# Split operands for the state's product in the chunk scan of a pooling and Mamba-2 step

## The chip, the cores and the metric

The kernel runs on one core of one Trainium2 chip, as one launch. The metric is the device time of that launch in microseconds (us). The core has a matrix engine (TensorE, PE in the profile), a vector engine (VectorE, DVE), an activation engine (ScalarE, ACT), a general engine (GpSimd, POOL) and an engine that here only issues DMAs (SyncE, SP). Each works through its own queue in order, and they meet at semaphores. Tiles lie in SBUF on 128 partitions; PE writes its products to PSUM banks of 128 x 512 float32 numbers.

## The reference

One layer of a hybrid decoder, for a prompt of 1024 rows and for 8 samples of 8 rows, 1024 wide. A normalised and modulated input goes through one projection; its parts feed a pooling branch and a state-space (SSD) branch, whose outputs are gated, summed and projected. The change lies in the SSD branch of the prompt. It has 32 heads of 64 channels in 4 groups of 8 heads; each group shares B and C (128 states). The 1024 rows are scanned in 8 chunks of 128:

```python
def step(h, inp):
    xq, dq, Bq, Cq = inp
    acs = jnp.cumsum(dq * Ag, axis=1)
    seg = acs[:, :, None] - acs[:, None, :]
    decay = jnp.exp(jnp.where(mask, seg, -jnp.inf))
    cb = jnp.einsum('bign,bjgn->bijg', Cq, Bq)
    att = cb[..., None] * decay * dq[:, None]
    y = jnp.einsum('bijge,bjgep->bigep', att, xq)
    y = y + jnp.einsum('bign,bige,bgepn->bigep', Cq, jnp.exp(acs), h)
    last = acs[:, -1]
    w_in = jnp.exp(last[:, None] - acs) * dq
    h = h * jnp.exp(last)[..., None, None] + jnp.einsum('bjgn,bjge,bjgep->bgepn', Bq, w_in, xq)
    return h, y
...
y = (y + d_skip.astype(jnp.float32)[:, None] * xs).reshape(b, L, D_INNER)
y = rmsnorm(y * jax.nn.silu(z_ssm.astype(jnp.float32)), ssm_norm_g)
s = y.astype(x.dtype) @ w_ssm_out
```

The state after the last chunk is an output too.

## The kernel before

All large products are made in split form: a float32 operand becomes a high part in the type fp32r and a low part, the rest, and the product is the sum of high x high, low x high and high x low. ACT makes the high part by a copy, DVE or GpSimd the low part by a subtraction.

**Stages.** The input is normalised, transposed and modulated (to about 90 us). Then the input projection runs in pairs of column tiles by a Strassen scheme (products on line 411, to about 758 us); beside it GpSimd and ACT split later weights, the convolution runs on DVE (line 1089), dt and its cumulative sums are made in `dt_end` (lines 1104 to 1205), and the 8 samples are scanned. The chunk stage follows (about 758 to 1045 us), then the last group's output products and the last projection with the final norm.

**The chunk stage.** 32 generators `chunk(g, c)` (line 1492), 4 groups by 8 chunks, one after the other. Each goes through five steps:

1. It issues its loads: `dec`, the cumulative sums of the group's 8 heads spread over all partitions; `bc` (B and C); `xb` (x, 4 tiles of 128 channels by 128 rows).
2. ACT makes `cE` (exponentials of the sums, line 1504), GpSimd masks `dec` (`far`, line 1229), and ACT turns it into decays, one instruction a head with the row's own sum as bias (`exps`, line 1233).
3. PE transposes x into the bank `px` (line 1511) and B into `pbc`, and makes the product of B and C there (lines 1513, 1514). ACT copies B's transpose to `bt` and, after the first chunk, C into PSUM (line 1518). DVE makes `xd` = x dt (line 1522) and `xw` = x weighted for the state (line 1524), and multiplies `dec` and `cE` by PSUM (lines 1529, 1531).
4. PE makes the state's increment `pu` = bt x xw (line 1536), a plain float32 product of 128 x 128 by 128 x 512, then `inner` (lines 1245, 1248): 8 heads of decays against `xd` and, after the first chunk, of `cE` against the state before. GpSimd decays the state (line 1542) and DVE adds `pu` (line 1544). DVE adds D x to the result in PSUM, four instructions with a scale for each channel (line 1548).
5. `finish` (line 1462): DVE multiplies by the gate `sz` (line 1464), ACT makes the high part and the squares, GpSimd the low part (line 1468) and sums of squares.

**Order.** The loop on line 1844 hands out the steps: in iteration i step 3 of chunk i + 1, some products, step 4 of chunk i, the loads of chunk i + 3 and of the gate, step 2 of chunk i + 2, step 5 of chunk i, one step of `wo_splits` (which splits the last projection's weights, lines 1766 to 1819), and more products. The products are 2.56 pieces an iteration of other branches' output projections (`gemm_`, line 221, 12 matmuls of 352 or 384 columns a piece, added up on DVE in line 1740 after the first group). From line 1834 on `in_line` fixes the program's order on PE and SP (at the start of the stage on ACT and DVE too); a scheduler with a timeline of its own orders ACT, DVE and GpSimd. `xw` has one buffer, `xd` and `bt` two, `xb` five, `sz` three; four PSUM banks (`PB`) go round for `px`, `pbc` and `inner`, and `pu` has one of its own (`PC`).

The functions that the change touches, and what calls them:

Of the kernel before, what the change touches and what calls it, by code (L numbers as in the profile page):

```python
# [8 lines left out]
F32 = mybir.dt.float32  # L9
F32R = mybir.dt.float32r  # L10
AF = mybir.ActivationFunctionType
# [9 lines left out]
P = 128  # L21
# [25 lines left out]
def tile_pool_ssd_step(  # L47
# [8 lines left out]
    def nm(s):  # L56
        uid[0] += 1
        return f"{s}_{uid[0]}"
# [1045 lines left out]
    def dt_end():  # L1104
# [86 lines left out]
        for c0 in (8, 0, 4):  # L1191
            cs = range(c0, min(c0 + 4, 9))
            n = sum(P if c < 8 else NS for c in cs)
            ps = PB()
            for c in cs:
                m = P if c < 8 else NS
                nc.tensor.transpose(ps[:NH, (c - c0) * P:(c - c0) * P + m], acT[:m, c, :], ident[:m, :m])
            if c0 == NC:
                Es[0] = sp.tile([P, 2, 512], F32, tag="h0", name="E", bufs=H0B)[:NH, 0, :NS]
                V.tensor_copy(Es[0], ps[:NH, :n])  # L1200
                store_(acS_d.rearrange("b h t -> h b t"), Es[0].rearrange("h (b t) -> h b t", t=8))
            else:
                at = sp.tile([P, 512], F32, tag="xd", name=nm("at"), bufs=2)[:NH]
                V.tensor_copy(at[:, :n], ps[:NH, :n])
                store_(acs_d[c0:c0 + 4].rearrange("c h t -> h c t"), at.rearrange("h (c t) -> h c t", t=P))

# [24 lines left out]
    def exps(dec, g, c):  # L1231
        for h in range(8):
            act(dec[:, h], dec[:, h], AF.Exp, bias=acT[:, c, 8 * g + h:8 * g + h + 1], scale=-1.0)  # L1233
# [225 lines left out]
    def ckt(shape, tag, bufs=2):  # L1459
        return (cl if tag in CKL else ca if tag in ("dec", "xb", "cE", "bc") else ck).tile(list(shape), F32, tag=tag, name=nm(tag), bufs=bufs)  # L1460
# [26 lines left out]
    def load_sz(j):  # L1487
        g, c = divmod(j, NC)
        szs.append(ckt([P, 4, P], "sz", 3))
        load(szs[-1], z_d[g][:, :, c * P:c * P + P])  # L1490

    def chunk(g, c):
# [6 lines left out]
        xb = ckt([P, 4, P], "xb", 5)  # L1499
# [15 lines left out]
        bt = ckt([P, P], "bt", 2)  # L1515
        act(bt, pbc[:, :P], AF.Copy)
        if c > 0:
            act(pbc[:, 2 * P:3 * P], Cf, AF.Copy)
# [3 lines left out]
        V.tensor_tensor(xd, pxv, dtT[:, c, heads].unsqueeze(2).to_broadcast([P, 8, 64]), ALU.mult)  # L1522
        xw = ckt([P, 8, 64], "xw", 1)
        V.tensor_tensor(xw, pxv, wdT[:, c, heads].unsqueeze(2).to_broadcast([P, 8, 64]), ALU.mult)
        if g == c == 0:
            yield
            far(dec, c)
            exps(dec, g, c)
        V.tensor_tensor(dec, dec, pbc[:, P:2 * P].unsqueeze(1).to_broadcast([P, 8, P]), ALU.mult)
# [6 lines left out]
        mm(pu, bt, xw.rearrange("p h d -> p (h d)"), start=True, stop=True)  # L1536
# [10 lines left out]
        for q in range(4):  # L1547
            V.scalar_tensor_tensor(pi[:, q], xb[:, q], Dv[:, 4 * g + q:4 * g + q + 1], pi[:, q], ALU.mult, ALU.add)
        yield
        finish(g, o, P, xb, szs.pop(0), pi)  # L1550
# [59 lines left out]
    def to_ssd():  # L1610
        nonlocal right, sd, sp, mask, maskS, blkS, dtT, acT, wdT, Elb, ElS
# [9 lines left out]
        Elb, ElS = one([P, NC, NH], "Elb"), one([P, NB, NH], "ElS")  # L1621
# [6 lines left out]
    sd = sp = mask = maskS = blkS = dtT = acT = wdT = Elb = ElS = None  # L1628
# [75 lines left out]
    for shape, tag, bufs in (((P, 512), "ph", 3), ((P, P), "bt", 2), ((P, 8, 64), "xd", 2), ((P, 8, 64), "xw", 1),  # L1704
                             ((P, 4, NS), "szs", 1), ((P, 512), "t2", 1), ((P, 512), "hst", 2)):
        ckt(shape, tag, bufs)
# [576 lines left out]
```

## Time and profile before

| what | us |
|---|---|
| median of 3 runs | 1211.38 |
| lowest and highest run | 1211.2, 1212.2 |
| the profiled execution | 1210.91 |
| its span, first to last instruction | 1209.2 |

The profile is of one execution. A page of it has the busy time of each engine, the chain of waits followed back from the last instruction, and groups of instructions. A group's row reads: line, engine, operation, output<-inputs, shapes, count | busy us, mean ns of one | idle time of the engine before them and what ended it. A row of the timeline reads: start us, duration us, engine, line, operation, tiles, shapes, count. The rows of one line give the least, median and largest duration in ns, and first and last start. Matmuls are pipelined and their ends are modelled: what one costs is the distance to the next start. PEld is the weight load beside PE.

### The profile page before, as it was taken

The numbers are of one execution on the slowest core, as the hardware profiler recorded it, in microseconds if no ns is written. First come the engines' busy times: TensorE is split into PE (matmuls) and PEld (weight loads), VectorE is DVE, ScalarE is ACT, GpSimd is POOL, SyncE is SP. The second block draws the span as 40 slices with busy tenths as digits, with TensorE's granted clock in tenths as the row PEclk, the third lists the DMA queues.
The fourth block names the chain that finished last, engine by engine and source line by source line (L and its number), as shares of the span: only waits on it lengthen the run. The fifth ranks groups of instructions, "written<-read, shape, count | busy, mean of one in ns | idle before, by whom it ended". The sixth has DMA issues, their size and how long they took to land.

```text
span 1209.2 us, 25239 instructions
## 1 busy us (share of the span) xinstructions
PE 1194.4 (99%) x9242; PEld 1118.5 (93%) x9242; DVE 924.8 (76%) x1535; ACT 649.1 (54%) x1479; POOL 763.4 (63%) x655
## 2 busy tenths in 40 slices
PE   9999999999999999999999999999999999999997
PEld 8879999999999999999989999988888888999885
DVE  6993788877989578877576555687878889679976
ACT  6864356565666557454434334566676657312435
POOL 1137878875988787764777776255767758423653
PEclk9999999999999999999999999999999999999999
DMA  9836445574556455454667767988879888585794
GB/s 352 306 132 219 136 144 184 164 228 146 171 174 198 160 164 172 135 169 131 208 227 238 245 223 247 320 309 262 270 250 294 277 284 285 173 326 166 235 212 154
DMA packets 167924, 262.72 MB, mean 217 GB/s; under 512 B 32880, under 2 KB 80760, under 8 KB 167800
## 3 DMA queue, kind: packets, MB, share of 16 engines
q1 hardware_dynamic: 90408, 166.01, 41.9%
q10 hardware_dynamic: 73232, 87.16, 21.2%
q0 software_dynamic: 4160, 7.94, 3.2%
q8 instruction: 73, 1.20, 0.4%
q14 instruction: 51, 0.42, 0.1%
HBM read 173.31 MB, written 87.73 MB: 216 GB/s over the span
## 4 chain that ended last, share of the span: by engine, by line
PE 87%; DVE 5%; DMA 3%; ACT 2%; issue 1%; POOL 0%; ACTq 0%; DVEq 0%; SPq 0%; POOLq 0%
PE mm L411 24%; PE ps L411 23%; PE mm L221 17%; PE pc L411 5%; PE ps L1245 3%; PE pc L1536 2%; PE ps L1248 2%; PE ps L2036 2%; PE ps L2034 2%; PE ps L2035 2%; PE ps L1511 1%; DMA dec<-acs_d 1%; DMA Y<-in_x_prompt 1%; PE ps L957 1%; DVE tf L643 1%
## 5 line engine op out<-in xcount | busy, mean ns | idle before, releaser
L148 POOL TENSOR_TENSOR wlo<-rawA,whi 128x512 fp32r<-128x512 f32 x120 | 174.7, 1461 | 80.7 <-ACT whi L145 79.4
L221 PE MATMUL mm<-Y,whi 128*128 128x352 f32 (+1 forms) x960 | 195.9, 334 | 0.8 <-DVE G L1969 0.6
L148 POOL TENSOR_TENSOR wlo<-raw,whi 128x512 fp32r<-128x512 f32 x90 | 149.8, 1673 | 64.6 <-ACT whi L145 62.2
L221 PEld LDWEIGHTS mm<-Y,whi 128*128 128x128 f32 x960 | 159.2, 188 | 7.6 <-issue 4.1
L1089 DVE SCALAR_TENSOR_TENSOR GA<-GA,cvT,GA 128x1112 f32<-128x1112 f32 x72 | 134.0, 1866 | 0.1
L411 PE MATMUL mm<-Y,whi 128*128 128x272 f32 x800 | 118.4, 290 | 0.0
L145 ACT ACTIVATE whi<-rawA 128x512 fp32r<-128x512 f32 x120 | 75.1, 627 | 79.6 <-PE ps L411 34.7
L411 PE MATMUL ps<-Y,whi 128*128 128x272 f32 x800 | 117.4, 289 | 0.0
L145 ACT ACTIVATE whi<-raw 128x512 fp32r<-128x512 f32 x90 | 56.0, 629 | 103.9 <-DVE raw L348 34.0
L411 PEld LDWEIGHTS mm<-Y,whi 128*128 128x128 f32 x800 | 106.9, 188 | 2.5 <-issue 1.0
L411 PEld LDWEIGHTS ps<-Y,whi 128*128 128x128 f32 x800 | 107.0, 188 | 0.8 <-issue 0.7
L221 PE MATMUL mm<-Y,wlo 128*128 128x352 f32 (+1 forms) x480 | 98.5, 327 | 0.0
L1233 ACT ACTIVATE dec<-dec,acT 128x128 f32<-128x128 f32 x256 | 78.8, 389 | 25.8 <-POOL dec L1229 25.8
L221 PEld LDWEIGHTS mm<-Y,wlo 128*128 128x128 f32 x480 | 81.7, 188 | 0.0
L286 POOL TENSOR_TENSOR pw<-pw,ph 128x512 fp32r<-128x512 f32 x40 | 67.0, 1675 | 13.4 <-ACT ph L284 12.5
L1468 POOL TENSOR_TENSOR Y<-xb,Y 128x512 fp32r<-128x512 f32 x32 | 41.2, 1287 | 53.7 <-ACT Y L1466 53.7
L411 PE MATMUL mm<-G,whi 128*128 128x272 f32 x480 | 71.2, 290 | 0.0
L411 PE MATMUL ps<-G,whi 128*128 128x272 f32 x480 | 70.3, 289 | 0.0
L411 PE MATMUL mm<-Y,wlo 128*128 128x272 f32 x400 | 66.8, 288 | 0.0
L411 PE MATMUL ps<-Y,wlo 128*128 128x272 f32 x400 | 66.6, 288 | 0.0
L411 PEld LDWEIGHTS mm<-G,whi 128*128 128x128 f32 x480 | 64.1, 188 | 1.2 <-issue 1.1
L411 PEld LDWEIGHTS ps<-G,whi 128*128 128x128 f32 x480 | 64.2, 188 | 0.3 <-issue 0.3
(579 smaller groups left out, 3130.5 us busy)
## 6 DMA issues: line engine op xcount, KB each, us to landing
rawA<-in_w_in SPq DMA_DIRECT2D x62, 512.0 KB
dec<-acs_d SPq DMA_DIRECT2D x32, 512.0 KB
xbc<-GA ACTq DMA_DIRECT2D x24, 512.0 KB
Y<-wo SPq DMA_DIRECT2D x10, 1024.0 KB
pw<-in_w_ssm_out ACTq DMA_DIRECT2D x32, 256.0 KB
ws<-ph ACTq DMA_DIRECT2D x32, 256.0 KB
ws<-pw ACTq DMA_DIRECT2D x32, 256.0 KB
h<-in_state_ssm SPq DMA_DIRECT2D x32, 256.0 KB
```

The lines of the kernel that those rows point to most:

```text
L145: ins = act(hi[:, :, :ncols], raw[:, :, :ncols], AF.Copy)
L148: (eng or nc.gpsimd).tensor_tensor(lo[:, :, :ncols], raw[:, :, :ncols], hi[:, :, :ncols].bitcast(F32), ALU.subtract)
L221: mm(ps[:, :n], w[k // 4][h][:, k % 4, :], r[k][:, o:o + n], start=(j == 0), stop=(j == len(terms) - 1))
L286: nc.gpsimd.tensor_tensor(raw.bitcast(F32R), raw, hi.bitcast(F32), ALU.subtract)
L411: mm(p, w[j // 8][:, k], A(k, s)[j // 4 == 1], start=(j == 0), stop=(j == 11))
L1089: V.scalar_tensor_tensor(d[:, :n], rp[:, k:k + n], cvT[:, 24 * k + mc:24 * k + mc + 1], d[:, :n], ALU.mult, ALU.add)
L1233: act(dec[:, h], dec[:, h], AF.Exp, bias=acT[:, c, 8 * g + h:8 * g + h + 1], scale=-1.0)
L1245: mm(o[hh], xd[:S, 2 * q + hh, :], dec[:S, 2 * q + hh], start=True, stop=state is None)
L1248: mm(o[hh], state[:, h * 64:h * 64 + 64], cE[:, h], start=False, stop=True)
L1468: nc.gpsimd.tensor_tensor(yl[g][:, :, o:o + S], v, yhc.bitcast(F32), ALU.subtract)
L1536: mm(pu, bt, xw.rearrange("p h d -> p (h d)"), start=True, stop=True)
L2034: mm(ps, hi, y[:, k, c0:c0 + cw], start=(first and k == 0), stop=False)
```

## The change

The state's product is made from split operands: `bt` and `xw` each become a high part in fp32r (`bt[:, 0]`, `xh`, by ACT) and a low part (`bt[:, 1]`, `xl`, by DVE), and three fp32r products add up in the same bank. dt leaves `xd`: the logarithm of dt, with dt at least 1e-37, is added to the cumulative sums in a new tile `alT` once, in `dt_end`, and the decays' exponentials take their bias from there, so that `xd` is a copy of `px`, made by ACT. For groups 0 and 1 GpSimd multiplies `xb` by D in place once it is transposed, and DVE adds the result of `inner` to it in one instruction; groups 2 and 3 keep the four scaled adds. The copy of C into PSUM moves behind `xh` on ACT. `sz` gets a fourth buffer, `xb` a sixth, and the order of the tiles in the pool `ck` changes.

```diff
--- before.py
+++ after.py
@@ -1203,6 +1203,10 @@
                 at = sp.tile([P, 512], F32, tag="xd", name=nm("at"), bufs=2)[:NH]
                 V.tensor_copy(at[:, :n], ps[:NH, :n])
                 store_(acs_d[c0:c0 + 4].rearrange("c h t -> h c t"), at.rearrange("h (c t) -> h c t", t=P))
+        al = alT.rearrange("p c h -> p (c h)")
+        V.tensor_scalar(al, dt[:, :256], 1e-37, None, ALU.max)
+        act(al, al, AF.Ln)
+        V.tensor_tensor(al, al, ac[:, :256], ALU.add)
 
     Es = [None, None]
 
@@ -1230,7 +1234,7 @@
 
     def exps(dec, g, c):
         for h in range(8):
-            act(dec[:, h], dec[:, h], AF.Exp, bias=acT[:, c, 8 * g + h:8 * g + h + 1], scale=-1.0)
+            act(dec[:, h], dec[:, h], AF.Exp, bias=alT[:, c, 8 * g + h:8 * g + h + 1], scale=-1.0)
 
     def load_E(E2, g):
         for hh in range(2):
@@ -1456,8 +1460,8 @@
 
     CKL = ("sz", "v")
 
-    def ckt(shape, tag, bufs=2):
-        return (cl if tag in CKL else ca if tag in ("dec", "xb", "cE", "bc") else ck).tile(list(shape), F32, tag=tag, name=nm(tag), bufs=bufs)
+    def ckt(shape, tag, bufs=2, dt=F32):
+        return (cl if tag in CKL else ca if tag in ("dec", "xb", "cE", "bc") else ck).tile(list(shape), dt, tag=tag, name=nm(tag), bufs=bufs)
 
     def finish(g, o, S, v, sz, y=None):
 
@@ -1486,7 +1490,7 @@
 
     def load_sz(j):
         g, c = divmod(j, NC)
-        szs.append(ckt([P, 4, P], "sz", 3))
+        szs.append(ckt([P, 4, P], "sz", 4))
         load(szs[-1], z_d[g][:, :, c * P:c * P + P])
 
     def chunk(g, c):
@@ -1496,7 +1500,7 @@
         bc = ckt([P, 2, P], "bc", 3)
         load(bc, xbc_d[g][c][:, 4:6])
         Bf, Cf = bc[:, 0], bc[:, 1]
-        xb = ckt([P, 4, P], "xb", 5)
+        xb = ckt([P, 4, P], "xb", 6)
         load(xb, xbc_d[g][c][:, 0:4])
         yield
         if c > 0:
@@ -1512,20 +1516,27 @@
         pbc = PB()
         nc.tensor.transpose(pbc[:, :P], Bf, ident)
         mm(pbc[:, P:2 * P], Bf, Cf, start=True, stop=True)
-        bt = ckt([P, P], "bt", 2)
-        act(bt, pbc[:, :P], AF.Copy)
-        if c > 0:
-            act(pbc[:, 2 * P:3 * P], Cf, AF.Copy)
+        bt = ckt([P, 2, P], "bt", 2, F32R)
+        act(bt[:, 0], pbc[:, :P], AF.Copy)
+        scaled = g < 2
+        if scaled:
+            nc.gpsimd.tensor_tensor(xb, xb, Dv[:, 4 * g:4 * g + 4].unsqueeze(2).to_broadcast([P, 4, P]), ALU.mult)
         pxv = px.rearrange("p (h d) -> p h d", d=64)
         heads = slice(8 * g, 8 * g + 8)
         xd = ckt([P, 8, 64], "xd", 2)
-        V.tensor_tensor(xd, pxv, dtT[:, c, heads].unsqueeze(2).to_broadcast([P, 8, 64]), ALU.mult)
-        xw = ckt([P, 8, 64], "xw", 1)
-        V.tensor_tensor(xw, pxv, wdT[:, c, heads].unsqueeze(2).to_broadcast([P, 8, 64]), ALU.mult)
+        act(xd, pxv, AF.Copy)
+        xw, xh, xl = ckt([P, 512], "xw", 1), ckt([P, 512], "xh", 2, F32R), ckt([P, 512], "xl", 2, F32R)
+        V.tensor_tensor(xw.rearrange("p (h d) -> p h d", d=64), pxv,
+                        wdT[:, c, heads].unsqueeze(2).to_broadcast([P, 8, 64]), ALU.mult)
+        act(xh, xw, AF.Copy)
+        if c > 0:
+            act(pbc[:, 2 * P:3 * P], Cf, AF.Copy)
         if g == c == 0:
             yield
             far(dec, c)
             exps(dec, g, c)
+        V.tensor_tensor(bt[:, 1], pbc[:, :P], bt[:, 0].bitcast(F32), ALU.subtract)
+        V.tensor_tensor(xl, xw, xh.bitcast(F32), ALU.subtract)
         V.tensor_tensor(dec, dec, pbc[:, P:2 * P].unsqueeze(1).to_broadcast([P, 8, P]), ALU.mult)
         if c > 0:
             V.tensor_tensor(cE, cE, pbc[:, 2 * P:3 * P].unsqueeze(1).to_broadcast([P, 8, P]), ALU.mult)
@@ -1533,7 +1544,9 @@
         if c == 0:
             yh[g], yl[g] = [Y4(hs if g % 2 else hp) for _ in range(2)]
         pu = PC()
-        mm(pu, bt, xw.rearrange("p h d -> p (h d)"), start=True, stop=True)
+        mm(pu, bt[:, 0], xh, start=True, stop=False)
+        mm(pu, bt[:, 1], xh, start=False, stop=False)
+        mm(pu, bt[:, 0], xl, start=False, stop=True)
         pi = inner(xd, dec, P, *((hst[g], cE) if c > 0 else ()))
         hn = ckt([P, 512], "hst", 2)
         if c == 0:
@@ -1544,10 +1557,13 @@
             V.tensor_tensor(hn, hn, pu, ALU.add)
         hst[g] = hn
 
-        for q in range(4):
-            V.scalar_tensor_tensor(pi[:, q], xb[:, q], Dv[:, 4 * g + q:4 * g + q + 1], pi[:, q], ALU.mult, ALU.add)
-        yield
-        finish(g, o, P, xb, szs.pop(0), pi)
+        if scaled:
+            V.tensor_tensor(xb, xb, pi, ALU.add)
+        else:
+            for q in range(4):
+                V.scalar_tensor_tensor(pi[:, q], xb[:, q], Dv[:, 4 * g + q:4 * g + q + 1], pi[:, q], ALU.mult, ALU.add)
+        yield
+        finish(g, o, P, xb, szs.pop(0), None if scaled else pi)
         if c == NC - 1:
             store_(new_ssm_p[g], hn)
 
@@ -1608,7 +1624,7 @@
         gas.append(right.__enter__())
 
     def to_ssd():
-        nonlocal right, sd, sp, mask, maskS, blkS, dtT, acT, wdT, Elb, ElS
+        nonlocal right, sd, sp, mask, maskS, blkS, dtT, acT, wdT, alT, Elb, ElS
         right.__exit__(None, None, None)
         sd_cm = tc.tile_pool(name="sd", bufs=1, side="right", reuse_waits="tile")
         sd = sd_cm.__enter__()
@@ -1618,14 +1634,14 @@
             return sd.tile(shape, F32, tag=name, name=name, bufs=1)
         mask, maskS, blkS = one([P, P], "mask"), one([NS, NB, 8], "maskS"), one([NS, NS], "blkS")
         dtT, acT, wdT = one([P, 9, NH], "dtT"), one([P, 9, NH], "acT"), one([P, 9, NH], "wdT")
-        Elb, ElS = one([P, NC, NH], "Elb"), one([P, NB, NH], "ElS")
+        alT, Elb, ElS = one([P, NC, NH], "alT"), one([P, NC, NH], "Elb"), one([P, NB, NH], "ElS")
         right = tc.tile_pool(name="sp", bufs=2, side="right", reuse_waits="tile")
         sp = right.__enter__()
         dt_steps.append(dt_end())
         next(dt_steps[0])
     dt_steps = []
     right_all = []
-    sd = sp = mask = maskS = blkS = dtT = acT = wdT = Elb = ElS = None
+    sd = sp = mask = maskS = blkS = dtT = acT = wdT = alT = Elb = ElS = None
 
     first()
 
@@ -1701,8 +1717,8 @@
     cl = open_("cl", 2)
     right = tc.tile_pool(name="ck", bufs=2, side="right", reuse_waits="tile")
     ck = right.__enter__()
-    for shape, tag, bufs in (((P, 512), "ph", 3), ((P, P), "bt", 2), ((P, 8, 64), "xd", 2), ((P, 8, 64), "xw", 1),
-                             ((P, 4, NS), "szs", 1), ((P, 512), "t2", 1), ((P, 512), "hst", 2)):
+    for shape, tag, bufs in (((P, 8, 64), "xd", 2), ((P, 2, P), "bt", 2), ((P, 512), "ph", 3), ((P, 4, NS), "szs", 1), ((P, 512), "t2", 1),
+                             ((P, 512), "hst", 2), ((P, 512), "xw", 1), ((P, 512), "xh", 2), ((P, 512), "xl", 2)):
         ckt(shape, tag, bufs)
 
     sq_acc = hs.tile([P, T], F32, tag="sq", name="sq_acc", bufs=1)

```

## Prediction

> **What bounds the kernel now.** I read first the page's busy shares and the engines of its chain of waits, then the four windows that cover the chunk stage (the only stage in which the change adds work to every step), then that stage's PE timeline.
>
> ```profile
> span 1209.2 us, 25239 instructions
> PE 1194.4 (99%) x9242; PEld 1118.5 (93%) x9242; DVE 924.8 (76%) x1535; ACT 649.1 (54%) x1479; POOL 763.4 (63%) x655
> ```
> ```profile
> PE 87%; DVE 5%; DMA 3%; ACT 2%; issue 1%; POOL 0%; ACTq 0%; DVEq 0%; SPq 0%; POOLq 0%
> ```
> ```profile
> 760.00:840.00 80.00, 79.75 (x623) 71.75 (x623) 62.67 (x109) 47.24 (x125) 36.34 (x42) 1.00 0.87 295
> 840.00:909.00 69.00, 69.00 (x557) 61.36 (x556) 52.86 (x82) 49.66 (x132) 47.72 (x57) 1.00 0.82 265
> 909.00:980.00 71.00, 70.64 (x565) 62.56 (x564) 59.80 (x107) 45.66 (x119) 53.33 (x62) 1.00 0.88 281
> 980.00:1045.00 65.00, 64.89 (x527) 57.26 (x526) 56.66 (x97) 35.10 (x91) 45.17 (x54) 1.00 0.83 270
> ```
>
> The window columns are stretch, sum, then PE, weight load, DVE, ACT and POOL with their counts, the granted clock, the DMA share and GB/s. The 32 chunks fill 760 to 1045 us, and PE is busy in 284.3 of those 285 us at clock 1.00. TensorE bounds the stage, so work taken off TensorE shortens the run, as long as no other engine is late. Next is DVE: 33.5 us of 149 are free in the first two windows (groups 0 and 1), but only 19.5 of 136 in the last two (groups 2 and 3).
>
> ```profile
> 883.36 0.80 PE L221 MATMUL mm<-Y,whi 128*128 128x352 f32 x4
> 884.00 1.02 PE L1536 MATMUL pc<-xw,bt 128*128 128x512 f32 x2
> 884.95 0.44 PE L1245 MATMUL ps<-dec,xd 128*64 128x128 f32 x4
> ...
> 892.68 0.44 PE L1245 MATMUL ps<-dec,xd 128*64 128x128 f32 x4
> ```
> ```profile
> 1097.89 0.39 PE L2034 MATMUL ps<-Y,a11h 128*128 128x512 f32 x1
> 1098.12 0.40 PE L2035 MATMUL ps<-Y,a11h 128*128 128x512 f32 x1
> 1098.35 0.40 PE L2036 MATMUL ps<-Y,a11l 128*128 128x512 f32 x1
> 1098.59 0.39 PE L2034 MATMUL ps<-Y,a11h 128*128 128x512 f32 x1
> 1098.82 0.86 PE L221 MATMUL mm<-Y,whi 128*128 128x384 f32 x4
> ```
>
> Matmuls overlap, so only the distances of starts count. The plain float32 product of L1536 appears as two records, and from its start (884.00) to the next line's start (884.95) pass 0.95 us. In the tail, split (fp32r) products of the same 128 x 512 size start every 0.93 / 4 = 0.232 us (1097.89 to 1098.82).
>
> **The state's product on PE.** One float32 product leaves and three fp32r products come. After the last comes L1245, whose tile is 128\*64 where L1536's is 128\*128. The 0.95 contains that changeover. Its two records are alike (1.02 us from the first start to the modelled end of the second, which is 0.59 long, so the second starts at 884.43):
>
> ```profile
> L1536 PE MATMUL pc<-xw,bt x64: 590/592/612, 772.1 to 1040.9; 128*128 128x512 f32 x64
> ```
>
> So a pass takes 0.43 us and the changeover 0.95 - 0.86 = 0.09. I leave the changeover in. After: 3 x 0.232 + 0.09 = 0.786 us for 0.95, a gain of 0.163 a chunk, and 32 x 0.163 = 5.2 us. Bounds: 0.25 a chunk if the changeover goes too (8.2 us), and nothing below 0.16, since the three terms are exactly what L2034 to L2036 do. The Trainium skill ("FP8 and Floating Point Precision", TensorE Precision Notes) says that true FP32 takes four passes through the array; four of 0.232 are an estimated 0.93 plus changeover, and the sum would be 32 x 0.232 = 7.4 us. The trace shows 0.86, so I keep 5.2.
>
> **DVE.** Durations:
>
> ```profile
> L1548 DVE SCALAR_TENSOR_TENSOR ps<-xb,Dv,ps 128x128 f32<-128x128 f32 x124 | 43.4, 350 | 4.5 <-PE ps L1248 2.4
> L1464 DVE TENSOR_TENSOR xb<-ps,sz 128x512 f32<-128x512 f32 x32 | 21.9, 686 | 0.6
> L1524 DVE TENSOR_TENSOR xw<-ps,wdT 128x512 f32<-128x512 f32 x30 | 20.5, 684 | 4.9 <-PE pc L1536 4.8
> L1522 DVE TENSOR_TENSOR xd<-ps,dtT 128x512 f32<-128x512 f32 x29 | 19.7, 680 | 0.8 <-PE ps L1511 0.8
> L1804 DVE TENSOR_TENSOR R<-t,R 128x512 f32<-128x512 f32 x4 | 4.7, 1164 | 0.0
> L1800 DVE TENSOR_TENSOR t<-R,R 128x512 f32<-128x512 f32 x4 | 3.8, 956 | 0.0
> L1793 DVE TENSOR_TENSOR R<-R,R 128x512 f32<-128x512 f32 x4 | 3.8, 939 | 3.6 <-DMA R<-in_w_o 3.6
> L1794 DVE TENSOR_TENSOR R<-R 128x512 f32<-128x512 f32 x4 | 2.8, 691 | 0.0
> ```
> ```profile
> L1290 DVE TENSOR_TENSOR xw<-ps,xw x4: 273/274/283, 575.8 to 693.2; 64x128 fp32r<-64x128 f32 x4
> ```
>
> Every chunk loses the dt product xd (0.68) and gains the low part of B (128 wide with a PSUM operand: 0.27 by L1290) and xl, both of whose operands lie in SBUF. Operations with a PSUM operand run at 0.68 to 0.69; those with SBUF operands alone, of the same size, average (1.164 + 0.956 + 0.939 + 0.691) / 4 = 0.94 in this stage. The long ones fell beside GpSimd:
>
> ```profile
> 996.83 1.50 DVE L1804 TENSOR_TENSOR R<-t,R 128x512 f32<-128x512 f32 x1
> ```
> ```profile
> 996.35 3.13 POOL L1773 TENSOR_TENSOR R<-R,ph 128x512 fp32r<-128x512 f32 x2
> ```
>
> The Trainium skill ("SBUF — State Buffer", SBUF: two separate sides) has the rule: a DVE operation with two SBUF inputs and a GpSimd operation that reads SBUF share a port pair, and the later one blocks until the other is done. This pair of rows agrees, and the rule speaks against the change, because xl and, for two groups, the gate product become such operations. By it an xl could wait out a whole GpSimd operation (an estimate of 0.68 + 1.1), and 16 of them would cost 13 us more than I count.
>
> I take 0.94, with ends 0.69 and 1.5. A chunk then gains 0.94 + 0.27 - 0.68 = 0.53 us of DVE. In groups 0 and 1 four scaled adds (4 x 0.35) become one add with a PSUM operand (0.69), and the gate product loses its PSUM operand (0.69 to 0.94): -0.46, so +0.07 in all. In groups 2 and 3 all of it stays: 16 x 0.53 = 8.5 us into 19.5 us of idle time. It lies beside PE, at no cost on average.
>
> **ACT and POOL.**
>
> ```profile
> L1466 ACT ACTIVATE Y<-xb 128x512 fp32r<-128x512 f32 x32 | 19.9, 623 | 20.8 <-DVE xb L1464 20.8
> L1540 ACT ACTIVATE hst<-pc 128x512 f32<-128x512 f32 x3 | 1.7, 581 | 0.0
> ```
> ```profile
> L1542 POOL TENSOR_TENSOR hst<-hst,Elb 128x512 f32<-128x512 f32 x27 | 28.9, 1072 | 10.2 <-DVE hst L1544 6.3 <-PE ps L1248 2.3 <-ACT hst L1540 1.6
> ```
>
> ACT gains the copy of px to xd (0.58 by L1540) and xh (0.62 by L1466): 32 x 1.2 = 38.4 us on 177.7 busy of 285, 216 of 280 after. POOL gains 16 times D x (1.07 by L1542, which also has a broadcast operand): 17 us on 84 of 149. Both stay off the path. The new waits: on ACT xh waits for DVE's xw, and the copy of C into PSUM stands behind it; on DVE xl waits for xh, and the products into dec and cE stand behind xl, for which PE waits; on POOL D x waits for PE's transposes, with the masking of the next dec behind it, for which ACT's exponentials wait. One wait goes: xw has one buffer, and DVE idled 4.8 us until PE had read it; now only xh and xl read it. What is late next is the pair xh, xl: 0.62 + 0.94 behind xw.
>
> Is there slack for that? An ordinary chunk and the tightest that I found:
>
> ```profile
> 887.92 1.21 DVE L1531 TENSOR_TENSOR cE<-cE,ps 128x1024 f32<-128x1024 f32 x1
> ```
> ```profile
> 1013.85 1.21 DVE L1531 TENSOR_TENSOR cE<-cE,ps 128x1024 f32<-128x1024 f32 x1
> ```
> ```profile
> 1014.08 1.02 PE L1536 MATMUL pc<-xw,bt 128*128 128x512 f32 x2
> 1015.21 0.44 PE L1245 MATMUL ps<-dec,xd 128*64 128x128 f32 x4
> ```
>
> The first cE is done at 889.13 and PE reaches it at 892.68: 3.5 us early, enough for 0.53 or 1.6. The second ends at 1015.06, and PE, which would start at 1015.03, starts at 1015.21. There the added 0.53 shows: I charge one such place, 0.18 + 0.53 = 0.7 us, with ends 0 and the rivals below. Only PE and the SP queue keep a written order here; where ACT, DVE and POOL put the new steps among the others no row tells.
>
> **The rest at nothing.** The step that ends dt gets a maximum, a logarithm and an add over 256 columns, and the logarithm wants a table:
>
> ```profile
> L1899 ACT ACT_TABLE_LOAD x1 | 1.3, 1283 | 0.0
> ```
> ```profile
> 560.00:580.00 20.00, 20.00 (x155) 18.93 (x154) 11.36 (x26) 14.60 (x29) 10.66 (x13) 1.00 0.45 125
> ```
>
> At most two loads and 0.4 us, 3.0 us on ACT, where ACT has 5.4 us of 20 free under a full PE; uncovered it would cost 3.0, at best it costs nothing. The exponentials take another bias of the same shape. The extra xb and sz buffers and the larger pool move no bytes; the first chunk could wait for the pool's space, but PE takes its product at 772.1 (L1536's row above), 12 us into the stage.
>
> **Sum.** Profiled execution 1210.91 (span 1209.2): -5.2 + 0.7 = -4.5, 1206.4. The median of the runs is 1211.38, 0.5 above, so 1206.9. A measurement here can tell 0.2% from no change, 2.4 us: faster lies below 1209.0, slower above 1213.8.
>
> **Rivals.** (1) *DVE takes most of it back.* For it: in the last two windows DVE has 1.2 us idle a chunk, and 0.53 plus the period's 0.16 come out of that. Against: slack of 3.5 us in the ordinary chunk. If half of the 8.5 us is uncovered, 1211.4 - 5.2 + 4.2 = 1210.4; the case spans 1209 to 1213.8. Here too belongs that loads hold the stage (DMA share 0.82 to 0.88), no change at 1211.4.
> (2) *DVE becomes the bound of groups 2 and 3: slower.* If its 19.5 us of idle time are waits that cannot be filled, the 16 chunks grow by all 8.5 us, and only groups 0 and 1 keep their 2.6: 1211.4 + 8.5 - 2.6 = 1217.3. It decides against the change once more than 5.2 of the 8.5 us is uncovered, or xl averages over 1.47 us (116.5 busy + 16 x 1.06 is PE's 133.4). For it: 1.50 us in the row at 996.83. Against: 0.94 on average. The Trainium skill's shared port pair, on its page on SBUF, is what would bring it about.
> (3) *More.* The changeover goes as well, 1203.2. By the four passes of the Trainium skill's page on precision the sum would be 1204.0 before stalls; the row's 0.86 speaks against it.
>
> **How the numbers follow.** Forecast 0.65 (its own range 1205.4 to 1208.9), more 0.05, rival 1 0.18, slower 0.12. Faster 0.70, same 0.18, slower 0.12. The range 1204.0 to 1212.5 takes in the forecast, most of more and most of rival 1, and leaves out the slower case and the edges.
>
> **What would show it.** Right: three L1536 records a chunk 0.23 us apart, 0.79 us to L1245, PE still without gaps, the chunk stage 4 to 5 us shorter, xl near 0.9. Wrong: PE waiting for DVE's xl, dec or cE in groups 2 and 3, DVE over 95% busy there, xl near 1.5, or a gap on PE at 560 to 580 us.

## The result, and the profile after

The change made the kernel slower: 1221.93 us median (1219.62 to 1223.45, 6 runs) against 1212.89 (1211.2 to 1214.41, 6 runs), a ratio of 1.0073, 95% interval 1.0063 to 1.0083. That is 9 us lost, where 4.5 were to be gained. The profiled execution took 1221.24 us, 10.3 more than that of before.

The page of the kernel after (span, busy times, the engines of its chain of waits):

```profile
span 1219.5 us, 25386 instructions
...
PE 1191.8 (98%) x9274; PEld 1126.1 (92%) x9274; DVE 934.9 (77%) x1521; ACT 680.1 (56%) x1545; POOL 794.4 (65%) x671
...
PE 72%; DVE 9%; DMA 6%; issue 5%; POOL 4%; ACT 4%; SPq 0%; ACTq 0%; DVEq 0%; POOLq 0%
```

PE has 2.6 us less to do in a span that is 10.3 us longer, and the chain runs through PE for 72% instead of 87%; DVE, loads (DMA), GpSimd, ACT and time in which no wait shows (issue) took its place. The windows of the chunk stage (columns as in the prediction):

```profile
760.00:840.00 80.00, 78.91 (x635) 73.63 (x634) 64.19 (x94) 54.84 (x141) 48.89 (x50) 1.00 0.88 298
840.00:909.00 69.00, 66.43 (x546) 61.20 (x543) 50.33 (x63) 55.39 (x142) 58.78 (x62) 0.98 0.78 255
909.00:980.00 71.00, 65.58 (x529) 60.49 (x527) 63.29 (x103) 50.97 (x128) 53.73 (x56) 1.00 0.83 262
980.00:1045.00 65.00, 63.06 (x532) 57.97 (x531) 57.12 (x103) 45.05 (x114) 45.40 (x51) 1.00 0.88 287
```

PE was idle 0.7 us in these 285; now it is idle 11.0. DVE is busy 63.29 of 71 and 57.12 of 65 us in the last two windows, 89 and 88%: it is not full. The waits of the stage (740 to 1070 us; engine, line, what it waited for: us in total, times, longest), first after:

```profile
DVE xw L1529 <- ACT xd L1527: 17.1, 13, 4.0
...
ACT xh L1531 <- DVE xw L1529: 9.8, 6, 2.7
PEld pc L1549 <- DVE xl L1539: 8.6, 4, 3.0
DVE bt L1538 <- ACT ps L1533: 8.5, 10, 2.0
...
PE pc L1549 <- DVE xl L1539: 6.9, 4, 2.6
...
DVE xl L1539 <- ACT xh L1531: 6.2, 5, 3.1
```

and the one before that the prediction said would go:

```profile
DVE xw L1524 <- PE pc L1536: 4.8, 8, 1.7
```

It went, and a wait of 17.1 us stands in its place: xw now waits for ACT's copy xd, from which it takes nothing. The two only read the same bank px; a different engine reads it for each, and the program orders them one behind the other. So the state's product hangs on a chain with five crossings between queues: from PE's transposes to xd on ACT, to xw on DVE, to xh on ACT, to xl on DVE, and back to PE. Before there were two: from the transposes to xw on DVE and back. The timeline shows one such chain late:

```profile
858.00 2.44 ACT L1237 ACTIVATE dec<-dec,alT 128x128 f32<-128x128 f32 x8
...
860.50 0.58 ACT L1527 ACTIVATE xd<-ps 128x512 f32<-128x512 f32 x1
...
864.85 0.63 ACT L1531 ACTIVATE xh<-xw 128x512 fp32r<-128x512 f32 x1 [2.19 <-DVE xw L1529]
...
862.95 1.27 DVE L1809 TENSOR_TENSOR R<-R,R 128x512 f32<-128x512 f32 x1 [2.90 <-DMA R<-in_w_o]
864.14 0.68 DVE L1529 TENSOR_TENSOR xw<-ps,wdT 128x512 f32<-128x512 f32 x1
...
867.79 1.21 DVE L1542 TENSOR_TENSOR cE<-cE,ps 128x1024 f32<-128x1024 f32 x1
868.92 0.67 DVE L1561 TENSOR_TENSOR xb<-xb,ps 128x512 f32<-128x512 f32 x1
869.51 1.53 DVE L1539 TENSOR_TENSOR xl<-xw,xh 128x512 fp32r<-128x512 f32 x1
...
868.13 0.40 PE L1548 MATMUL pc<-xh,bt 128*128 128x512 f32 x1
871.10 0.50 PE L1549 MATMUL pc<-xl,bt 128*128 128x512 f32 x1 [2.57 <-DVE xl L1539]
```

ACT takes up xd after eight exponentials. In DVE's queue L1809 stands ahead of xw, and DVE waits there 2.90 us for a load. ACT then idles 2.19 us for xw. xh is there at 865.48, but six steps stand between xw and xl in DVE's queue, dec, cE and L1561 among them, and xl itself takes 1.53 us. PE stands for 2.6 us between the second product and the third.

PE waited for xl in four of the 32 chunks. From the timeline, in us:

| chunk (from 0) | xd done, xw starts | of it DVE waited for xd | xh done, xl starts | DVE's steps meanwhile | PE waited for xl |
|---|---|---|---|---|---|
| 11 | 861.08, 864.14 | 0 | 865.48, 869.51 | L1816, bt, dec, cE, L1561 | 2.57 |
| 19 | 936.26, 936.29 | 0.83 | 938.18, 940.42 | dec, cE | 1.41 |
| 21 | 954.06, 954.09 | 0.42 | 956.12, 960.04 | L1816, bt, dec, cE | 2.23 |
| 23 | 974.09, 974.12 | 0.09 | 978.35, 980.29 | dec, cE | 0.68 |

In three of them xw starts as soon as xd is done, so a late xd makes a late xw. But only 1.3 of the 17.1 us of waits for xd fall here, and in all four 1.9 to 4.0 us pass between xh and xl, mostly with the products into dec and cE (1.21 us each). The source issues xl ahead of those two; in the queue it stands behind dec in 22 of 32 chunks, as the scheduler placed it.

**The sum.** Worked out over all chunks (distances between starts of neighbouring matmuls beyond the median of that pair of lines, where they exceed it by 0.17 us, from 755 to 1052 us), PE's gaps grew from 1.3 us to 13.5: 7.5 ahead of the state's products, 2.7 inside `inner` (dec, cE), 1.9 ahead of the transpose of B, 1.3 at the stage's entry. A stretch at half clock behind the gap at 868 cost 1.7 more (last section). The stage before, where no instruction of PE differs, began 1.3 us later (first product of L411 at 91.9 against 90.6; 89.4 to 92.0 in the profiles of all kernels here). -5.2 + 12.2 + 1.7 + 1.3 = 10.0 of the 10.3 us.

### The profile page after: what moved, and what is told of

The parts are those of the page before. It is cut to its first block, busy times and chain, and to the rows that moved or that the text cites. A ratio compares the mean times of both kernels' runs of the same rounds, so it can differ in the third digit from the quotient of the medians.

```text
span 1219.5 us, 25386 instructions
## 1 busy us (share of the span) xinstructions
PE 1191.8 (98%) x9274; PEld 1126.1 (92%) x9274; DVE 934.9 (77%) x1521; ACT 680.1 (56%) x1545; POOL 794.4 (65%) x671
## 4 chain that ended last, share of the span: by engine, by line
PE 72%; DVE 9%; DMA 6%; issue 5%; POOL 4%; ACT 4%; SPq 0%; ACTq 0%; DVEq 0%; POOLq 0%
PE mm L411 23%; PE ps L411 23%; PE mm L221 10%; PE pc L411 5%; PE ps L1249 2%; ACT dec L1237 1%; PE ps L1252 1%; DMA R<-in_x_sample 1%; DVE G L1991 1%; DMA R<-gs 1%; PE ps L957 1%; DMA Y<-in_w_gate 1%; DVE tf L643 1%; POOL R L1789 1%; PE ps L1515 1%
## 5 line engine op out<-in xcount | busy, mean ns | idle before, releaser
L411 PE MATMUL mm<-Y,whi 128*128 128x272 f32 x800 | 118.5, 290 | 0.0
L411 PE MATMUL ps<-Y,whi 128*128 128x272 f32 x800 | 117.4, 289 | 0.0
L411 PEld LDWEIGHTS mm<-Y,whi 128*128 128x128 f32 x800 | 106.9, 188 | 2.5 <-issue 1.8
L411 PEld LDWEIGHTS ps<-Y,whi 128*128 128x128 f32 x800 | 107.0, 188 | 0.8 <-issue 0.7
L1237 ACT ACTIVATE dec<-dec,alT 128x128 f32<-128x128 f32 x256 | 78.8, 390 | 33.8 <-POOL dec L1233 33.8
L411 PE MATMUL mm<-G,whi 128*128 128x272 f32 x480 | 71.3, 290 | 0.0
L411 PE MATMUL ps<-G,whi 128*128 128x272 f32 x480 | 70.3, 289 | 0.0
L411 PE MATMUL mm<-Y,wlo 128*128 128x272 f32 x400 | 66.8, 288 | 0.0
L411 PE MATMUL ps<-Y,wlo 128*128 128x272 f32 x400 | 66.6, 288 | 0.0
L411 PEld LDWEIGHTS mm<-G,whi 128*128 128x128 f32 x480 | 64.1, 188 | 1.2 <-issue 1.1
L411 PEld LDWEIGHTS ps<-G,whi 128*128 128x128 f32 x480 | 64.2, 188 | 0.3 <-issue 0.3
```

The costliest lines, as they stand in the source:

```text
L411: mm(p, w[j // 8][:, k], A(k, s)[j // 4 == 1], start=(j == 0), stop=(j == 11))
L1237: act(dec[:, h], dec[:, h], AF.Exp, bias=alT[:, c, 8 * g + h:8 * g + h + 1], scale=-1.0)
```

## Experiments

Theory, *late chain*: TensorE's gain is there, and the loss is lateness, xl behind the crossings that xw's wait for xd starts. Rival, *work*: DVE and ACT have too much to do in groups 2 and 3, whatever the order. The scheduler orders ACT, DVE and GpSimd anew for each version, so an edit of one line can move other steps too, or move nothing. Diffs are against the changed kernel unless another is named; ratios are to the kernel before, run on the same chip.

**xw ahead of xd.**

```diff
-        act(xd, pxv, AF.Copy)
         V.tensor_tensor(xw.rearrange("p (h d) -> p h d", d=64), pxv, ...)
+        act(xd, pxv, AF.Copy)
```

> The changed kernel with one line moved: DVE reads the bank of transposed x for xw first, and ACT's copy to xd comes behind it. Theory (a late chain): in the change xw waits for ACT's copy of the same bank (17 us of idle DVE time, 13 times), and xh, xl and the third product wait behind it; without that wait PE's waits for xl (8.6 us on its weight loads) fall below 4 us and the run is 3 to 7 us shorter than the change. Rival (DVE has too much work in groups 2 and 3): DVE's work is the same, so the run stays within 2 us of the change.

Measured: 1215.12 us, ratio 1.0026 (1.0011 to 1.0041). 5.7 of the 9 us come back without an operation less. The waits of this kernel:

```profile
DVE xl L1539 <- ACT xh L1531: 13.5, 9, 4.9
...
PE ps L1249 <- DVE cE L1542: 3.3, 2, 2.6
```

No wait of xw for ACT is left. The scheduler's order of DVE changed with the line: xl stands behind dec in 10 of 32 chunks instead of 22, so the gain is that of both. PE's gaps at the state's products fall from 7.5 to 0.9 us, but those in `inner` grow from 2.7 to 5.9: part of the lateness moved on to cE.

**xd = x dt on DVE again,** with no logarithm and acT as the decays' bias. Both readers of px are then on one engine.

```diff
-        act(xd, pxv, AF.Copy)
+        V.tensor_tensor(xd, pxv, dtT[:, c, heads].unsqueeze(2).to_broadcast([P, 8, 64]), ALU.mult)
```

> The changed kernel without the dt part: xd = x dt on DVE again, the decays' bias is the plain cumulative sum, no logarithm. Late chain: no engine but DVE reads the bank of transposed x, xw waits for PE alone, and although DVE gets 32 x 0.68 = 22 us more the run is shorter than the change by 3 to 8 us. Rival (DVE's amount of work): 0.68 us a chunk more on an engine with about 1 us idle a chunk in groups 2 and 3, so 5 us or more longer than the change.

Measured: 1215.38, ratio 1.0026 (1.0008 to 1.0044). The same gain although DVE is busy 12 us more (947.3 against 934.9); xl stands behind dec in 16 of 32 chunks. This speaks for the chain and against DVE's work.

**D x on DVE in all groups.**

```diff
-        scaled = g < 2
+        scaled = False
```

> The changed kernel with D x on DVE in all four groups, none on GpSimd. Late chain: the waits of groups 2 and 3 (8 of the 12 us) stay as they are, the one wait of group 1 may go, so 0 to 3 us shorter than the change. Rival (GpSimd's 16 extra operations and the gate product with two SBUF operands hold DVE up): 5 us or more shorter.

Measured: 1221.15, ratio 1.0064 (1.0044 to 1.0083), the change's time; xw waits 19.4 us for xd. GpSimd's part is not the cause. It has one small price, at the stage's entry, where GpSimd's first D x falls beside DVE's two subtractions. The timeline after, and then of this run:

```profile
764.09 1.08 PE L221 MATMUL mm<-Y,whi 128*128 128x384 f32 x5 [1.09 <-DVE Y L1583]
...
760.71 3.33 DVE L1583 TENSOR_TENSOR Y<-Y,Y 128x1088 fp32r<-128x1088 f32 x2
...
760.84 2.05 POOL L1523 TENSOR_TENSOR xb<-xb,Dv 128x512 f32<-128x512 f32 x1 [1.63 <-PE ps L1515]
```
```profile
760.99 1.08 PE L221 MATMUL mm<-Y,whi 128*128 128x384 f32 x5 [0.25 <-DVE Y L1583]
...
758.45 2.49 DVE L1583 TENSOR_TENSOR Y<-Y,Y 128x1088 fp32r<-128x1088 f32 x2
```

Side by side the subtractions take 3.33 us instead of 2.49, and PE waits 0.84 us longer. Here the rule of the Trainium skill ("SBUF — State Buffer", SBUF: two separate sides), that a DVE operation with two SBUF inputs and a GpSimd operation that reads SBUF exclude each other, agrees with the trace; it is worth 0.8 us of the 9.

**dt in the exponents alone:** the plain float32 product, D x on DVE, the copy xd on ACT and the logarithm kept.

```diff
-        mm(pu, bt[:, 0], xh, start=True, stop=False)
-        mm(pu, bt[:, 1], xh, start=False, stop=False)
-        mm(pu, bt[:, 0], xl, start=False, stop=True)
+        mm(pu, bt[:, 0], xw, start=True, stop=True)
```

> Only the dt part of the change: the state's product is plain float32 again (no xh, xl, low part of B), D x on DVE in all groups, xd is ACT's copy, the logarithm is there. Late chain: xw still waits for ACT's copy, but nothing but PE stands behind it, so PE's gaps in the chunk stage stay under 3 us; with the product's 5.2 us not gained the run is at 1212 to 1217 where before has 1212.9. Rival (amount of work on DVE): 0.68 us a chunk less than before on DVE, so the time of before or 1 us less; an entry cost of the logarithm would show as a gap of up to 3 us at 560 to 580 us.

Measured: 1213.24, ratio 1.0006 (0.9994 to 1.0019): no difference. The logarithm, the bias and the copy cost nothing by themselves. xw waits 10.2 us for xd here too, and PE's gaps are 2.4 us: with xw as the product's own operand the chain is two crossings shorter, and most of the slack holds.

**No xl.** The third product takes xh again, so that TensorE's work stays and the low part of xw is missing from the state.

```diff
-        V.tensor_tensor(xl, xw, xh.bitcast(F32), ALU.subtract)
...
-        mm(pu, bt[:, 0], xl, start=False, stop=True)
+        mm(pu, bt[:, 0], xh, start=False, stop=True)
```

> The changed kernel without the low part xl: DVE's subtraction is left out and the third product takes xh a second time, so PE's work is unchanged and the state's low part is missing. Late chain: PE's waits at the third product (8.6 us on its weight loads) and the halved clock behind the longest of them go; the waits for dec and cE stay: 7 to 11 us shorter than the change, 1211 to 1215 where before has 1212.4. Rival (DVE's amount of work): 32 x 0.94 = 30 us less on DVE, so all waits go and the run lies at the 5.2 us that PE saves, 1207 to 1209.

Measured: 1216.27, ratio 1.0025 (1.0013 to 1.0037). DVE is busy 22 us less (912.8 against 934.9), and that gives back what the swap of two lines gives, not more. Both expectations are missed, the rival's by 7 us and the late chain's by 1: xw still waits 26.4 us for xd, and PE, freed of xl, stops in `inner` (4.7 us of 6.9).

**`inner` ahead of the state's products** (the line that makes `pi` moves above the three), in the changed kernel, with xw first, and with xd on DVE.

> The changed kernel with PE's two steps exchanged: the products of inner come before the state's three, so that xl may come 1.9 us later without a wait; every engine has the same work. Late chain: the waits at the third product (2.7, 1.6, 2.4, 0.8 us) shrink by up to 1.9 us each and the halved clock goes, while inner is taken 0.8 us earlier and waits a little more for dec and cE: 3 to 7 us shorter than the change. Rival (amount of work on DVE): no change, within 2 us, the waits only move to another product.

> The first experiment and the exchange of inner and the state's product together: xw ahead of ACT's copy, inner ahead of the three products. Late chain: PE's waits in the chunk stage fall under 4 us, so 1210 to 1214, level with before. Rival (amount of work on DVE): as the first experiment alone, 1215.

> xd = x dt on DVE with no logarithm (the second experiment) and inner ahead of the three products. Late chain: 1210 to 1214; the waits that are left are for dec and cE, behind which DVE's 0.68 us a chunk for xd stands. Rival (amount of work on DVE): no better than the second experiment, 1215.

Measured: 1216.28, ratio 1.0032 (1.0019 to 1.0045); with xw first 1214.0, 1.0008 (0.9993 to 1.0024), no different from before; with xd on DVE 1216.9, 1.003 (1.0013 to 1.0047). The gaps at the state's products all but vanish (0.4, 0, 0 us), those in `inner` rise to 8.6, 7.7 and 6.9. The late chain's time came in the first, and in the second at its edge, but there with 8.9 us of gaps where under 4 were expected. In the third the rival's line came true: it is no better than xd on DVE alone.

**More products between the transposes and the state's product,** in the changed kernel and with xw first.

```diff
-        products(i + 0.4)
+        products(i + 0.8)
```

> The change as it is, but 0.4 of an iteration's products of other branches that follow the state's products now stand ahead of them: about one more piece (0.4 x 2.56 = 1.0 piece of 12 matmuls, about 2 us) lies between a chunk's transposes and its state product. No work is added or removed. Late chain: xl has 2 us more, and most of the gaps ahead of the third state product (2.74, 1.57, 2.39, 0.84 us in the change) close; what is left is other waits: 1213 to 1217 us. Rival (ACT and DVE simply have too much to do in groups 2 and 3): shifting the product by 2 us moves the waits and does not remove them: 1220 to 1223 us.

> xw ahead of ACT's copy xd, and the piece of products more between a chunk's transposes and its state product. Late chain: both parts of the lateness shrink, the gaps fall under those of the run with xw first alone (5.7 us of the 9 were given back there), and the gain of TensorE shows: 1207 to 1212 us. Rival (the waits for dec and cE take the place of those for xl, whatever the order): 1214 to 1217 us as with xw first alone.

Measured: 1218.55, ratio 1.004 (1.0027 to 1.0054), and 1219.22, 1.006 (1.0038 to 1.0082). The first falls between the expectations: waits of PE for xl disappear (7.5 to 0.2 us at the state's products), but the gaps ahead of the transpose of B, which needs a free PSUM bank, grow from 1.9 to 4.6 us; 4.1 of them are one wait for DVE's product into cE, which reads a bank. The second is as bad, worse than the rival expected: here xw first gave nothing back.

**xh by DVE, with xw first.** No crossing is left between xw and xl.

```diff
-        act(xh, xw, AF.Copy)
+        V.tensor_copy(xh, xw)
```

> xw ahead of xd, and DVE makes the high part xh itself: xw, xh and xl then lie on one engine, and no crossing to ACT is left in the state's path; DVE gets 32 x about 0.6 us = 19 us more, ACT as much less. Late chain: the crossings cost, so in spite of the work it is no slower than xw first alone (1212 to 1215 us). Rival (DVE's work in groups 2 and 3 is what is short): 16 x 0.6 us more on an engine 88% busy there show as delay, 1218 to 1224 us.

Measured: 1215.04, ratio 1.001 (1.0001 to 1.002). The last two windows of this kernel:

```profile
909.00:980.00 71.00, 67.33 (x556) 61.81 (x555) 68.74 (x115) 48.69 (x127) 57.85 (x61) 1.00 0.85 272
980.00:1045.00 65.00, 64.30 (x526) 59.22 (x526) 63.75 (x115) 39.65 (x99) 46.17 (x52) 1.00 0.88 280
```

DVE is busy 97% of groups 2 and 3 (132.5 of 136 us), against 89% in the change, and this is one of the fastest versions. Shortage of DVE time is refuted as the cause of the 9 us.

**The split in groups 0 and 1 alone, with xw first.** Groups 2 and 3 make the plain product, without xh and xl.

```diff
+        if g < 2:
             mm(pu, bt[:, 0], xh, start=True, stop=False)
...
+        else:
+            mm(pu, bt[:, 0].bitcast(F32), xw, start=True, stop=True)
```

> xw ahead of xd, and the split product only in groups 0 and 1, where DVE has room; groups 2 and 3 make the plain float32 product of the kernel before (with dt in the decays and xd copied by ACT). TensorE keeps half of its gain, 16 x 0.163 = 2.6 us. Late chain: groups 2 and 3 have no xh and xl to wait for, so the gaps there shrink to those of the kernel before, and the time is 1209 to 1212 us against 1212.4 before. Rival (it is the moved copy xd on ACT and the decays' new bias that delay groups 2 and 3): 1214 to 1217 us.

Measured: 1219.43, ratio 1.0051 (1.0037 to 1.0065). A miss: worse than xw first in all groups. Of its 9.0 us of gaps 2.6 lie between 868 and 880 us (group 1), where the others have some too, and 2.6 at 973 us, in group 2, where nothing is split. There ACT took the next chunk's exponentials ahead of its copy of C into PSUM and of xd; DVE waited 3.05 us for the one and PE 2.45 for the bank that xd reads. Since the change had moved the copy of C, four runs put it back behind the copy of B.

**The copy of C in its old place,** in the half split, with xh by DVE, in the change itself, and with xh by DVE and `inner` first.

```diff
         act(bt[:, 0], pbc[:, :P], AF.Copy)
+        if c > 0:
+            act(pbc[:, 2 * P:3 * P], Cf, AF.Copy)
...
-        if c > 0:
-            act(pbc[:, 2 * P:3 * P], Cf, AF.Copy)
```

> Split product in groups 0 and 1 alone with xw ahead of xd, as before (1219.4 us), and ACT's copy of C into PSUM back in its old place, right behind the copy of B. Theory (the moved copy of C is a wait of its own: the product into dec shares its bank and stood 3.05 us behind it at 974.7, under exponentials of the next chunk): the 2.6 us gap at 973 and part of the others go, 1211 to 1215 us. Rival (the copy's place does not matter, the two engines are late anyway): 1218 to 1220 us.

> xw ahead of xd and xh made by DVE (1215.0 us), and the copy of C back in its old place. Theory (late copy of C): DVE's 8.8 us of waits for it in the chunk stage shrink and the time falls to 1210 to 1213 us, at or under the kernel before. Rival: 1214 to 1216 us.

> The change as it is with only the copy of C back in its old place. Theory that both late steps matter (xw behind xd, and C behind xh): DVE's waits for C (8.5 us) shrink, the waits of xw for xd stay, and 1 to 4 of the 9 us come back: 1217 to 1220 us. Rival one (C is the whole cause): 1210 to 1213 us. Rival two (C is none of it): 1220 to 1223 us.

> xw first, xh by DVE, copy of C in its old place, and the products of inner ahead of the state's three, so that xl is needed some 1.8 us later. If what is left is lateness of xl: 1207 to 1210 us. If it is dec and cE that come late: as without the last edit or 1 us slower, since PE then reaches dec 0.8 us sooner.

Measured: 1216.69, ratio 1.0032 (1.0021 to 1.0044); 1215.94, 1.0027 (1.0014 to 1.0039); 1221.03, 1.0057 (1.0043 to 1.0072); 1214.46, 1.0012 (1.0002 to 1.0022). In the change, and with xh by DVE, the edit did not reach the chip: in the traces ACT, DVE and GpSimd run the same instructions in the same order as without it. These two runs say nothing about the copy's place. They are repeats, and show what a repeat is worth: 1.0073 and 1.0057, 1.0010 and 1.0027, 2 us each time. In the half split, where the order did change, 2.3 us come back by the ratios, which the intervals do not set apart from nothing, and the gap near 970 stays. With `inner` first the second of the two outcomes came: 6.1 us of gaps for cE. The timeline of the half split:

```profile
969.22 2.14 ACT L1237 ACTIVATE dec<-dec,alT 128x128 f32<-128x128 f32 x7
971.27 0.26 ACT L1522 ACTIVATE ps<-bc 128x128 f32<-128x128 f32 x1
...
971.76 0.57 ACT L1532 ACTIVATE xd<-ps 128x512 f32<-128x512 f32 x1
...
971.63 1.22 DVE L1542 TENSOR_TENSOR dec<-dec,ps 128x1024 f32<-128x1024 f32 x1 [2.70 <-ACT ps L1522]
...
972.39 0.48 PE L1517 MATMUL ps<-ident,bc 128*128 128x128 f32 x1 [2.09 <-ACT xd L1532]
```

The line that issues the copy moved, but in ACT's queue it still stands behind seven exponentials of the next chunk: the scheduler that orders ACT put it there. And PE waits for xd itself, which holds the bank that the next transpose wants.

**DVE's steps in TensorE's order:** as the last of these, with the products into dec and cE ahead of xh, the low part of B and xl; then also D x on DVE in all groups.

> As the last run (xw first, xh by DVE, copy of C in its old place, inner ahead of the state's products; 1214.5 us), and DVE's products into dec and cE now stand ahead of xh, the low part of B and xl: each step comes in the order in which TensorE asks for it. If the order of DVE's queue is what is left of the loss: 1209 to 1212 us, under the kernel before. If the queues are late whatever the order (exponentials behind GpSimd's masking, loads, wo_splits): 1213 to 1216 us.

> The run above with D x on DVE in all groups. At the stage's entry GpSimd's first D x (2.05 us at 760.84 in the change) ran beside DVE's two low-part subtractions, which took 3.33 us there against 2.49 us in the run without GpSimd's D x, and TensorE waited 1.09 us against 0.25. That 0.84 us goes; DVE gets 16 x about 1 us of work back in groups 0 and 1. Sum if that work is hidden: 0.8 us less than the run above. If it is not: 1 to 4 us more.

Measured: 1218.39, ratio 1.0044 (1.0026 to 1.0061), and 1217.07, 1.0029 (1.0015 to 1.0042). Slower than without the edit (1.0012); 8.6 us of gaps in `inner`. But the order to be tested did not come about: in both traces xh and xl still stand ahead of dec in 25 of 32 chunks, as without the edit, and mainly the low part of B moved, to behind cE. Whether TensorE's order would help stays untested. Taking GpSimd's D x away removes the gap at the entry (1.3 to 0.4 us) as expected.

PE's gaps of the chunk stage beside the ratios, in us:

| kernel | ratio | all gaps | state's products | `inner` | transpose of B |
|---|---|---|---|---|---|
| before | 1 | 1.3 | 0 | 0.2 | 0.7 |
| the change | 1.0073 | 13.5 | 7.5 | 2.7 | 1.9 |
| xw first | 1.0026 | 8.1 | 0.9 | 5.9 | 0 |
| xd on DVE | 1.0026 | 9.4 | 0.8 | 5.9 | 1.1 |
| no xl | 1.0025 | 6.9 | 0 | 4.7 | 0.7 |
| xw and `inner` first | 1.0008 | 8.9 | 0 | 7.7 | 0 |
| xw first, xh by DVE | 1.0010 | 8.5 | 0 | 2.6 | 3.2 |
| more products between | 1.0040 | 12.1 | 0.2 | 1.9 | 4.6 |
| dt in the exponents alone | 1.0006 | 2.4 | 0 | 1.2 | 0.7 |

The gaps are of one execution, the ratios of medians. The gaps less 6.5 us (5.2 of gain, 1.3 of before; 1.3 alone for dt in the exponents), with 1.7 for a stretch at half clock in the stage, come within 1 us of what the ratio says, but for "xw and `inner` first" (3.1 us over) and "more products between" (2.4 over).

**Shown:** the loss is waits of PE in the chunk stage, and the stretch at half clock behind one of them; with the later start the sum closes to 0.3 us. In the change's order, putting xw ahead of xd, or xd back on DVE, gives back 4 to 6 us (from 1.0073, 1.0057 in the repeat, to 1.0026 both times). DVE's amount of work did not cost it, nor GpSimd's D x (but for 0.8 us) or the logarithm. **Shown too:** with the split in place in all groups, PE keeps 6.9 to 9.4 us of gaps in the better orders, which eat its 5.2 us; closing them at one place opens them at another (xl, then cE, then the banks). No version beat the kernel before. **Not shown:** how much of the 4 to 6 us is xw's wait for xd and how much the place of xl in DVE's queue, which the scheduler changed with it; and the effect of the copy of C's place in the change. **Open:** whether a better order exists. Every version leaves ACT's and DVE's queues to the scheduler, whose order often did not follow the edits; an order for them written by hand was not tried.

## Why the prediction was wrong

The step that failed is the one on the new waits, as the prediction put it: "One wait goes: xw has one buffer, and DVE idled 4.8 us until PE had read it; now only xh and xl read it. What is late next is the pair xh, xl: 0.62 + 0.94 behind xw." That counts the chain from xw on, and only durations. It starts one step earlier, with ACT's xd, whose wait the list of new waits lacks: 17.1 us on DVE. And xl does not follow xh: at the four places where PE waited for it, it started 1.9 to 4.0 us after xh was done, because the products into dec and cE stood ahead of it in DVE's queue, where the prediction had them "behind xl". The missing wait could be read off the diff: two instructions on two engines read `pxv`, where one engine read it twice before. The Trainium skill ("PSUM — Partial Sum Buffer", PSUM bank collisions raise a hardware error) says that accesses of two engines to one bank have to be kept apart, reads against reads included; the trace agrees, with 13 waits of xw for xd after and none before. That rule spoke against the change and was not weighed.

- **TensorE's gain: right.** An ordinary chunk after, on PE:

```profile
858.40 0.39 PE L1547 MATMUL pc<-xh,bt 128*128 128x512 f32 x1
858.63 0.40 PE L1548 MATMUL pc<-xh,bt 128*128 128x512 f32 x1
858.86 0.40 PE L1549 MATMUL pc<-xl,bt 128*128 128x512 f32 x1
859.19 0.44 PE L1249 MATMUL ps<-dec,xd 128*64 128x128 f32 x4
```

  0.23 us apart and 0.79 from the first to L1249, as forecast. A chunk with 36 products of other branches and no gap takes 9.48 us at the least, where it took 9.65.
- **Durations: right or high.** The lines of xl, bt's low part and xd (least, median, largest in ns):

```profile
L1539 DVE TENSOR_TENSOR xl<-xw,xh x32: 681/851/1677, 769.0 to 1047.7; 128x512 fp32r<-128x512 f32 x32
```
```profile
L1538 DVE TENSOR_TENSOR bt<-ps,bt x32: 275/284/293, 768.9 to 1045.2; 128x128 fp32r<-128x128 f32 x32
```
```profile
L1527 ACT ACTIVATE xd<-ps x32: 571/582/603, 761.4 to 1039.5; 128x512 f32<-128x512 f32 x32
```

  0.85, 0.28 and 0.58 us, where 0.94, 0.27 and 0.58 were taken; the mean of xl is 0.93.
- **The slack: wrong.** "3.5 us early, enough for 0.53 or 1.6" was read from one ordinary chunk and set against durations. What came was not 1.6 us but a chain in which every crossing between two queues may wait for what stands ahead in them: 4.0, 2.7 and 3.1 us at the longest in the rows of the waits. One charged place of 0.7 us stands against 7.5 us at the state's products and 4.6 at `inner` and the transposes.
- **Rival 2** had the sign and, at 1217.3, was nearest, but its mechanism is refuted: DVE at 88 and 89%, xl's mean 0.93 us instead of over 1.47, and a version with DVE at 97% loses 0.1% (0.3% in the repeat). Its row of 1.50 us does point at something real: xl waits for GpSimd (last section), which at the four late places is 1.4 of the 6.9 us that PE waited for xl.
- **Rest at nothing:** the logarithm is hidden (PE 20.00 of 20 us from 560 to 580, and no difference for dt alone). GpSimd's D x was not quite nothing: 0.84 us at the entry.
- **The range** was set from amounts of work; its upper end, 1212.5, held no case in which waits, not work, take the gain.

## What to carry to other kernels

When an edit moves one of two readers of a PSUM bank to another engine, count a new wait between the two, and follow the chain from PE back to PE: here the number of crossings between queues, and what stood ahead in each, mattered more than the sum of durations. Slack read from the last step (cE ready 3.5 us early) is not slack of a chain that has three more crossings. Where a scheduler orders the queues, compare the order in the traces before and after an edit: two of the edits here changed nothing on the chip, and one did not make the order that it was to test. Moving the late step made the next one late in this stage: sum the gaps of the bottleneck engine by what they wait for before choosing the next edit.

## What the runs showed of the hardware

TensorE's clock halved after gaps that were well under 3.4 us. The windows around the gap at 868 after (the gap, then what follows it) and around that of the run with xw first at 1017:

```profile
868.20:871.10 2.90, 0.33 (x3) 0.00 (x1) 2.90 (x4) 2.90 (x12) 2.90 (x4) 1.00 0.60 228
871.70:875.10 3.40, 3.40 (x33) 3.07 (x31) 2.83 (x6) 2.46 (x6) 2.71 (x3) 0.50 0.22 82
```
```profile
1017.00:1020.50 3.50, 0.91 (x6) 0.47 (x6) 2.60 (x3) 2.19 (x6) 3.50 (x5) 1.00 1.00 361
1020.50:1024.00 3.50, 3.50 (x33) 3.17 (x33) 3.49 (x7) 3.40 (x11) 0.49 (x2) 0.51 0.10 36
```

The granted clock is 0.50 for about 3.4 us behind the gap, which costs 1.7 us more than the gap itself. In the profiles of all kernels here, all 8 gaps of over 2.6 us from the input projection on were followed by such a stretch (twice as long in two of them), and 10 of the 44 between 1.3 and 2.6 us. The Trainium skill ("TensorE: Matmul & The Clock Gate", Part 1: The HAM clock gate) describes a free-running window of 3413 ns after which an idle array is halved; the length of the slow stretch agrees, but its rule of no gaps over about 3.4 us (HAM oscillation — how this bites in real kernels) is too wide here: 1.5 us was the shortest gap followed by half clock.

xl, a subtraction on DVE with both operands in SBUF, waited for the GpSimd operation that was running when it started. For the xl at 869.51 in the timeline of the change:

```profile
869.23 1.27 POOL L1789 TENSOR_TENSOR R<-R,ph 128x512 fp32r<-128x512 f32 x1
```

GpSimd's operation ends at 870.50, 0.98 us after xl starts, and xl takes 0.98 + 0.55 = 1.53 us. All 32 xl of the change follow this to 0.01 us: what is left of GpSimd's operation plus 0.55 us, and 0.68 us at the least. Twenty of them are held; together the 32 take 7.9 us more than 0.68 each.
